# Moving the attention layer's splits and the rotation's sine products from GpSimd to VectorE

## The chip, the cores and the metric

One core of a Trainium2 chip runs the whole program. The metric is device time in microseconds (us), here of three runs of each kernel. Besides these there is one profiled execution, from which all rows of this document come. The engines are PE (TensorE, matmul; PEld is its weight load), DVE (VectorE), ACT (ScalarE), POOL (GpSimd) and SP (SyncE, which only issues DMAs here).

## The reference, cut to what matters

Two layers of a diffusion transformer over 1024 latent tokens and 256 context tokens, 1024 channels, all in fp32. The first layer mixes by a Fourier transform and gated linear attention, the second by grouped-query attention with rotary positions; each ends with a convolutional feed-forward block. The change touches only the second layer's attention:

```python
q_l = apply_rope(attn_q(a_lat, w_q, g_q[j]), cos, sin)
k_l, v_l = attn_kv(a_lat, w_kv, g_k[j])
k_l = apply_rope(k_l, cos, sin)
k_c, v_c = attn_kv(a_ctx, w_kv, g_k[j])
...
s = jnp.einsum('bkgqd,bksd->bkgqs', q, k).astype(jnp.float32) * (HEAD_DIM ** -0.5)
p = jax.nn.softmax(s, axis=-1).astype(v.dtype)
...
o_lat = ob.transpose(1, 0, 4, 2, 3, 5).reshape(B_, S, Q_WIDTH) @ w_att_out[j]
...
def apply_rope(t, cos, sin):
    t1, t2 = jnp.split(tf, 2, axis=-1)
    return jnp.concatenate([t1 * cos - t2 * sin, t1 * sin + t2 * cos], axis=-1).astype(t.dtype)
```

There are 8 query heads and 2 key/value heads of 128 channels; `attn_q` and the keys also pass an RMS norm per head.

## The kernel before

Every matmul factor is held as two fp32r parts, hi and lo, and each product is three matmuls (`mm3`, L518). The parts come from `split` (L206): ScalarE rounds the source to hi (the CAST on L208), then one subtraction gives lo, on VectorE unless the caller names GpSimd (`G`). All two-tensor operations are issued by the helper `tt`, so they stand on L204 in the profile whoever calls them.

```python
def tt(out_, a, b, op, eng=None):
    return (eng or V).tensor_tensor(out_, a, b, op)

def split(src, hi, lo, eng=None):
    A.copy(hi, src)
    return tt(lo, src, hi.bitcast(F32), ALU.subtract, eng)
```

The attention layer runs in this order; the times are from the span's start in the profiled execution.

- **Up to about 1692.** The first layer's feed-forward block ends. `att_split` (L1706) splits the normed input of one half of the tokens (640 columns, 8 channel blocks), its even blocks on GpSimd and its odd ones on VectorE. The keys and values of the first half follow.
- **1692 to 1831, the projection.** `kv` (L1795) and `q_all` (L1830) make keys and queries two heads at a time. `tok_w` (L536) loads and splits the weights, two pieces of 128x1024 per set, their lo on GpSimd. `heads2` (L1738) then works block by block: for each of its tiles of 128 tokens (3 tiles for queries of the first half, 5 elsewhere) 24 matmuls of 256 columns on TensorE; the copy and squares on ScalarE (L1748, L1750); the inverse root of all tiles' sums (L386 to L395, with a square root on ScalarE in between); per tile two scalings by it on VectorE (L1758), two products with the sines on GpSimd (L1762, L1763), two with the cosines and two sums on VectorE (L1764 to L1767); then two transposes per tile on TensorE (L1772). `staged` (L1776) issues the matmuls of a block ahead of the rest of the block before it. `parts` (L1802) splits the finished keys and values, 128x1280 each, their lo on GpSimd. `att_split` of the second half runs ahead of the fourth query block.
- **1831 to 2200, the attention.** For each of 8 heads and 2 query halves `att_open` (L1870) loads 512 queries and splits them, lo on GpSimd. `att_a` (L1883) makes scores, the maximum on VectorE (L1894), the exponential on ScalarE (L1896) and the final scaling on GpSimd (L1905); `att_b` (L1909) transposes the weights, splits them from PSUM on ScalarE and VectorE, and multiplies by the values.
- **Twice, near 2010 to 2075 and 2200 to 2280,** `att_out` (L1939) makes the output projection: 8 weight pieces of 128x1024, loaded and split by `Wt` (L215), lo on GpSimd, each with 24 matmuls of 512 columns. The second one overlaps the preparation of the next feed-forward block (`Norm.scale`, `ffn_ops`, `Up.split`), part of which is on GpSimd before and after the change.

No order is written by hand here. Each engine has one queue that it works off in order, and a list scheduler with priorities of the program's stretches (`stream`, L169) settles it when the program is built; a new placing of an operation thus moves its neighbours too. Pools of fixed slots (`S` of 31, `W` of 10) limit how far loads run ahead. All loads named here are issued on SP's queue.

Of the kernel before, what the change touches and what calls it, by code (L numbers as in the profile page):

```python
# [20 lines left out]
P = 128  # L21
# [83 lines left out]
def tile_hybrid_dit(  # L105
# [100 lines left out]
# [4 lines that stand above are left out]
# [1496 lines left out]
    def att_split(hf):  # L1706
        for k in range(KT):
            a_t[hf][k] = b = S((2, HALF), True)
            split(hp[hf][k // 2][:, k % 2], b[:, 0], b[:, 1], (G, V)[k % 2])
            if k % 2:  # L1710
                hp[hf][k // 2].free()
            yield
# [25 lines left out]
    def heads2(c, tiles, w2, gi, put):  # L1738

        a = a_get(c)  # L1740
        nt = len(tiles)
        us = []
        ss = SM(2 * nt)
        for i, t in enumerate(tiles):
            ps = tok_chunk(a, w2, t)
            u = S((4, 2, P))
            us.append(u)
            A.copy(u[:, 0], ps.rearrange("p (h d) -> p h d", h=2))  # L1748
            for h in range(2):
                A.activation(u[:, 3, h], ps[:, h * P:(h + 1) * P], AF.Square, scale=P ** -0.5,  # L1750
                             accum_out=ss[:, 2 * i + h:2 * i + h + 1])
        yield
        rst = SM(2 * nt)
        rsqrt(ss, 2 * nt, rst)
        for i, (t, u) in enumerate(zip(tiles, us)):
            q, o, w = u[:, 0], u[:, 1], u[:, 2]
            for h in range(2):
                V.scalar_tensor_tensor(q[:, h], q[:, h], rst[:, 2 * i + h:2 * i + h + 1], gqk[:, gi], ALU.mult, ALU.mult)  # L1758
            g = c * NT + t - 2
            if g >= 0:  # L1760
                cs, sn = [rope[:, g, j, :].unsqueeze(1).broadcast_to([P, 2, 64]) for j in range(2)]
                tt(w[:, :, 0:64], q[:, :, 64:P], sn, ALU.mult, G)  # L1762
                tt(w[:, :, 64:P], q[:, :, 0:64], sn, ALU.mult, G)  # L1763
                tt(o[:, :, 0:64], q[:, :, 0:64], cs, ALU.mult)  # L1764
                tt(o[:, :, 64:P], q[:, :, 64:P], cs, ALU.mult)
                tt(o[:, :, 0:64], o[:, :, 0:64], w[:, :, 0:64], ALU.subtract)
                tt(o[:, :, 64:P], o[:, :, 64:P], w[:, :, 64:P], ALU.add)  # L1767
        yield
        for h in range(2):
            ps = banks((4, 4), nt * P, 1 if nt <= 4 else 2)  # L1770
            for i, (t, u) in enumerate(zip(tiles, us)):
                PE.transpose(ps[:, i * P:(i + 1) * P], u[:, 1 if c * NT + t >= 2 else 0, h], ident)  # L1772
            put(h, ps)
        free(*us)
# [10 lines left out]
    with stream(8):  # L1785
        rt = S(1280)
        rope = rt[:, 0:1024].rearrange("p (g i d) -> p g i d", g=8, i=2)
        gqk = rt[:, 1024:1280].rearrange("p (i d) -> p i d", i=2)
        nc.scalar.dma_start(rope, k_rope)
        nc.scalar.dma_start(gqk[:, 0], g_q[0].partition_broadcast(P))  # L1790
        nc.scalar.dma_start(gqk[:, 1], g_k[0].partition_broadcast(P))
        k_f = [S(TOK) for _ in range(2)]
        v_f = [S((5, 256)) for _ in range(2)]

        def kv(c):  # L1795
            def put(h, ps):
                A.copy(k_f[h][:, c * HALF:(c + 1) * HALF], ps)
            wk = tok_w(w_qkv_v, 1024, 256, G)
            yield from heads2(c, range(NT), wk, 1, put)
            free(*wk)  # L1800

        def parts(b):  # L1802
            hi, lo = S(TOK, True), S(TOK, True)
            split(b.a, hi.a, lo.a, G)
            b.free()
            return hi, lo

        def v_w():
            return tok_w(w_qkv_v, 1280, 256, G)

        def vv(c, wv):
            for t in range(NT):
                ps = tok_chunk(a_get(c), wv, t)
                A.copy(v_f[c][:, t, :], ps)
            free(*wv)
            v_s.append(parts(v_f[c]))

        def q_block(i, w2, c):
            tiles = range(2, NT) if c == 0 else range(NT)
            n = len(tiles) * P  # L1820
            st = S((2, n))

            def put(h, ps):
                A.copy(st[:, h], ps)
            yield from heads2(c, tiles, w2, 0, put)
            o = HALF - CTX if c else 0
            DMA(qS[2 * i:2 * i + 2, :, o:o + n].rearrange("h p c -> p h c"), st.a)
            st.free()

        def q_all(c):  # L1830
            for i in range(4):
                w2 = tok_w(w_qkv_v, 256 * i, 256, G)
                if c == 0 and i == 3:
                    run(att_split(1))
                yield q_block(i, w2, c)
                free(*w2)

        run(a_gen)
        k_s, v_s = [], []
        def kv_q():  # L1840
            yield kv(1)
            q = q_all(1)
            yield next(q)
            k_s.extend(parts(b) for b in k_f)
            yield from q

        g = kv(0)
        next(g)
        wv = v_w()
        run(att_side(n_att[1]))  # L1850
        vv(0, wv)
        run(g)
        staged(q_all(0))
        free(*a_t[0])
        staged(kv_q())
        rt.free()
# [13 lines left out]
    def att_open(qb, h):  # L1870
        B = Blk()
        B.kv, B.h, B.qb = h // 4, h, qb
        if h % 2 == 0:
            o_s[qb, h // 2] = (S((2, 512), True), S((2, 512), True))
        qr = W(512)
        DMA(qr.a, qS[h, :, qb * 512:(qb + 1) * 512])
        B.qs = W((2, 512), True)
        split(qr.a, B.qs[:, 0], B.qs[:, 1], G)
        qr.free()
        B.pr, B.po = {}, {}  # L1880
        return B
# [57 lines left out]
    def att_out(qb, between=lambda n: None):  # L1939
# [4 lines left out]
        for n in range(KT):  # L1944
            if n % 2 == 0:
                DMA(hp[qb][n // 2].a, hS[n * P:(n + 2) * P, qb * 512:(qb + 1) * 512].rearrange("(k p) c -> p k c", p=P))
            h = hp[qb][n // 2][:, n % 2]
            w = Wt(w_ao_v[:, :, n * P:(n + 1) * P], (KT, P), G)
            ps = banks(TO, 512, 1)
            for k in range(KT):  # L1950
                oh, ol = o_s[qb, k // 2]
                mm3(ps, (w.hi[:, k, :], w.lo[:, k, :]), (oh[:, k % 2], ol[:, k % 2]), k == 0, k == KT - 1)
            w.free()
            V.scalar_tensor_tensor(h, ps, mods[:, 1, 2, n, 0:1], h, ALU.mult, ALU.add)
            dump("h3", h, (n, slice(None), slice(CTX + qb * 512, CTX + (qb + 1) * 512)))
            N.sq(n, N.acc_b.a, W)
            if n % 2:
                h_store(h3_d, qb, n // 2, 512)
            between(n)
# [147 lines left out]
```

## Time and profile before

| | us |
|---|---|
| runs (3): median, lowest to highest | 3030.18, 3023.17 to 3033.33 |
| profiled execution, its own time | 3020.81 |
| its span in the trace | 3018.9 |
| busy in the span: PE | 2770.2 |
| DVE | 2344.4 |
| ACT | 1440.7 |
| POOL | 985.9 |

The profiled execution lies 9.4 us under the median of the runs and 1.9 us over its span. The page gives busy time by engine; the views of the trace give the same for a stretch, for one line and shape, or in order of time. In such rows "idle before" is the time that the engine stood still just ahead of the instruction, with what released it. TensorE runs at a granted clock (PEclk, 1.00 is 2.4 GHz, its other level is 1.2 GHz), so a stretch at 0.90 has lost a tenth of its length to the clock.

### The profile page before, as it was taken

To read this page: it belongs to the slowest core of one execution; us is meant where nothing else is said; L and a number is where in the kernel's file an instruction comes from. 1 tells how busy PE (TensorE), PEld (TensorE's weight loads), DVE (VectorE), ACT (ScalarE), POOL (GpSimd) and SP (SyncE) were. 2 spreads that over 40 slices of the span, in tenths; PEclk is the share of its full clock that TensorE was granted. 3 is DMA by queue.
4 is the path that set the end of the run, shared out by engine and by line. 5 is a ranking of instruction groups with operands and counts; after the bars stand their busy time and mean duration, and the time that the engine had idled before them with its cause. 6 is when DMAs were issued, how large, how long until landed. Compare 5 with 4: busy or idle time off the path is not lost. (4 is left out here: it accounts for less than half of the span.)

```text
span 3018.9 us, 50383 instructions
## 1 busy us (share of the span) xinstructions
PE 2770.2 (92%) x19189; PEld 2601.9 (86%) x19189; DVE 2344.4 (78%) x4065; ACT 1440.7 (48%) x2892; POOL 985.9 (33%) x843
## 2 busy tenths in 40 slices
PE   5999988797899999999999889999987999999898
PEld 4899977797798999989899888998977999998677
DVE  7897479768877766677894788876878888888885
ACT  3544433535544444453354545764755455455343
POOL 2025275104332222123233654343344333232211
PEclk7999978998899999999899999999998999999999
DMA  8553302332343333459753220012042222227973
GB/s 282 183 159 104 114 32 79 96 127 66 99 127 124 128 121 116 131 173 305 230 172 126 88 88 29 15 58 73 12 123 68 80 85 74 78 81 230 289 242 111
DMA packets 375784, 371.18 MB, mean 123 GB/s; under 512 B 15579, under 2 KB 305011, under 8 KB 375540
## 3 DMA queue, kind: packets, MB, share of 16 engines
q1 hardware_dynamic: 374482, 365.88, 38.0%
q8 instruction: 151, 2.47, 0.3%
q10 hardware_dynamic: 1058, 2.07, 0.2%
q14 instruction: 93, 0.76, 0.1%
HBM read 282.95 MB, written 84.93 MB: 122 GB/s over the span
## 5 line engine op out<-in xcount | busy, mean ns | idle before, releaser
L154 PE MATMUL psum<-t,t 128*128 128x320 f32 (+4 forms) x17038 | 2575.5, 311 | 159.5 <-DVE t L204 88.4
L154 PEld LDWEIGHTS psum<-t,t 128*128 128x128 f32 x17038 | 2412.0, 194 | 286.0 <-DVE t L204 105.0
L204 POOL TENSOR_TENSOR t<-t,t 128x512 fp32r<-128x512 f32 (+8 forms) x499 | 736.4, 1492 | 1124.7 <-ACT t L208 856.9
L204 DVE TENSOR_TENSOR t<-t,t 128x512 fp32r<-128x512 f32 (+12 forms) x997 | 829.5, 863 | 195.2 <-ACT t L208 87.0
L208 ACT CAST t<-t 128x512 fp32r<-128x512 f32 (+5 forms) x857 | 553.2, 672 | 589.3 <-DVE t L204 185.8
L204 DVE TENSOR_TENSOR t<-t,psum 128x320 f32<-128x320 f32 (+5 forms) x408 | 201.8, 516 | 43.8 <-ACT t L1310 21.2
L204 DVE TENSOR_TENSOR t<-t 128x512 f32<-128x512 f32 (+3 forms) x263 | 164.8, 646 | 45.4 <-DMA t<-in_w_ffn_down_dram 31.7
L204 POOL TENSOR_TENSOR t<-t 128x320 f32<-128x320 f32 (+2 forms) x120 | 124.0, 1067 | 225.0 <-ACT t L664 157.2
L208 ACT CAST t<-psum 128x512 fp32r<-128x512 f32 (+4 forms) x248 | 130.9, 536 | 134.8 <-PE psum L158 60.2
L158 PE MATMUL psum<-ident,t 128*128 128x128 f32 (+2 forms) x955 | 151.1, 280 | 39.5 <-DVE t L204 23.5
L204 DVE TENSOR_TENSOR t<-psum,t 128x512 fp32r<-128x512 f32 (+4 forms) x248 | 151.4, 615 | 37.6 <-ACT t L208 34.7
L1316 POOL COPY halo<-t 128x4 f32<-128x4 f32 x44 | 8.3, 188 | 472.6 <-DVE t L204 472.6
L1905 POOL TENSOR_SCALAR t<-t,ring 128x640 f32<-128x640 f32 x128 | 101.7, 808 | 168.7 <-DVE ring L1895 79.1
L158 PEld LDWEIGHTS psum<-ident,t 128*128 128x128 f32 (+2 forms) x955 | 113.3, 143 | 48.9 <-DVE t L204 27.7
L1328 ACT ACTIVATE t<-t,cvs 128x639 f32<-128x639 f32 (+3 forms) x176 | 152.3, 866 | 0.6 <-issue 0.6
L918 DVE SCALAR_TENSOR_TENSOR t<-psum,mods,t 128x320 f32<-128x320 f32 (+3 forms) x182 | 88.3, 513 | 42.7 <-PE psum L154 39.8
L1894 DVE TENSOR_REDUCE ring<-psum 128x1 f32<-128x640 f32 x128 | 104.5, 818 | 19.4 <-PE psum L154 13.6
L1327 ACT ACTIVATE t<-t 128x511 f32<-128x511 f32 (+3 forms) x88 | 60.5, 688 | 119.1 <-DVE t L1332 93.4
L1896 ACT ACTIVATE t<-psum,ring 128x640 f32<-128x640 f32 x128 | 102.3, 800 | 23.8 <-DVE ring L1902 11.2
L1300 ACT COPY t<-psum 128x320 f32<-128x320 f32 (+1 forms) x88 | 35.3, 401 | 150.7 <-DVE t L204 102.4
L1336 DVE SCALAR_TENSOR_TENSOR t<-t,cvs,t 128x255 f32<-128x255 f32 (+1 forms) x66 | 54.0, 845 | 66.7 <-ACT t L1328 66.7
L1310 ACT COPY t<-psum 128x320 f32<-128x320 f32 (+1 forms) x88 | 35.1, 398 | 122.9 <-PE psum L154 122.7
(145 smaller groups left out, 1690.8 us busy)
## 6 DMA issues: line engine op xcount, KB each, us to landing
t<-in_w_ffn_up_dram SPq DMA_DIRECT2D x98, 512.0 KB, 3.9
ring<-in_w_mod_dram SPq DMA_DIRECT2D x56, 512.0 KB, 3.8
t<-in_w_ffn_down_dram SPq DMA_DIRECT2D x96, 256.0 KB, 6.0
t<-in_w_even_in_dram SPq DMA_DIRECT2D x28, 512.0 KB, 4.9
t<-in_w_ffn_down_dram SPq DMA_DIRECT2D x72, 192.0 KB, 2.7
t<-y_d SPq DMA_DIRECT2D x20, 640.0 KB, 6.4
t<-in_w_mod_dram SPq DMA_DIRECT2D x96, 128.0 KB, 2.2
t<-in_w_ffn_down_dram SPq DMA_DIRECT2D x24, 512.0 KB, 4.4
```

The costliest lines, as they stand in the source:

```text
L154: cls.keep(out_, nc.tensor.matmul(out_, *args, **kw).ins)
L158: cls.keep(out_, nc.tensor.transpose(out_, *args).ins)
L204: return (eng or V).tensor_tensor(out_, a, b, op)
L208: A.copy(hi, src)
L918: last_resid[0] = V.scalar_tensor_tensor(h[:, n % 2, a:b], ps[:, a - c0:b - c0], mods[:, l, m, n, v:v + 1], h[:, n % 2, a:b], ALU.mult, AL ...
L1300: copied[:] = [A.copy(C(0, 0), ps)]
L1327: order(copied[0], A.activation(us[0], us[0], AF.Silu))
L1328: order(copied[0], A.activation(x, c[:, j, at:at + m], AF.Identity, bias=tap(l, 3, ft), scale=tap(l, 1, ft)))
L1336: V.scalar_tensor_tensor(x[:, s0 + 1:e], c[:, j, 2 + s0:1 + e], tap(l, 0, ft), x[:, s0 + 1:e], ALU.mult, ALU.add)
L1894: V.tensor_reduce(mx[:, i:i + 1], ps, AX.XY, ALU.max)
L1896: A.activation(pt[:, i * HALF:(i + 1) * HALF].rearrange("p (b n) -> p b n", b=2), ps, AF.Exp, bias=nb[:, i:i + 1], scale=SCALE, accum_out= ...
L1905: G.tensor_scalar(pt[:, i * HALF:(i + 1) * HALF], pt[:, i * HALF:(i + 1) * HALF], ex[:, i:i + 1], 1.0, ALU.mult, ALU.mult)
```

## The change

Ten places drop the engine `G`, so that the subtraction or product goes to VectorE: 40 lo parts of weights of 128x1024 (24 pieces of the projection, 16 of the two output projections), 8 of the layer's input of 128x640, 4 of keys and values of 128x1280, 16 of queries of 128x512, and 80 products with the sines (two for each of 40 tiles of 128 tokens). Their casts on ScalarE, their loads and all arithmetic stay. In the attention layer GpSimd keeps the 128 scalings of L1905.

```diff
     def att_split(hf):
         for k in range(KT):
             a_t[hf][k] = b = S((2, HALF), True)
-            split(hp[hf][k // 2][:, k % 2], b[:, 0], b[:, 1], (G, V)[k % 2])
+            split(hp[hf][k // 2][:, k % 2], b[:, 0], b[:, 1])
...
-                tt(w[:, :, 0:64], q[:, :, 64:P], sn, ALU.mult, G)
-                tt(w[:, :, 64:P], q[:, :, 0:64], sn, ALU.mult, G)
+                tt(w[:, :, 0:64], q[:, :, 64:P], sn, ALU.mult)
+                tt(w[:, :, 64:P], q[:, :, 0:64], sn, ALU.mult)
...
-            wk = tok_w(w_qkv_v, 1024, 256, G)
+            wk = tok_w(w_qkv_v, 1024, 256)
...
-            split(b.a, hi.a, lo.a, G)
+            split(b.a, hi.a, lo.a)
...
-            return tok_w(w_qkv_v, 1280, 256, G)
+            return tok_w(w_qkv_v, 1280, 256)
...
-                w2 = tok_w(w_qkv_v, 256 * i, 256, G)
+                w2 = tok_w(w_qkv_v, 256 * i, 256)
...
-        split(qr.a, B.qs[:, 0], B.qs[:, 1], G)
+        split(qr.a, B.qs[:, 0], B.qs[:, 1])
...
-            w = Wt(w_ao_v[:, :, n * P:(n + 1) * P], (KT, P), G)
+            w = Wt(w_ao_v[:, :, n * P:(n + 1) * P], (KT, P))
```

GpSimd's queue around the first query blocks of the projection. A row names what is written and read: t_15484 is the lo part of the third block's first weight piece, t_15481 its raw values and t_15483 its hi; t_15284, t_15312 and t_15340 are the work tiles of the first block's three token tiles, t_14865 the table of cosines and sines.

```order
-L204 TENSOR_TENSOR t_15484<-t_15481,t_15483 128x1024
-L204 TENSOR_TENSOR t_15284<-t_15284,t_14865 128x2x64 x2
-L204 TENSOR_TENSOR t_15490<-t_15487,t_15489 128x1024
-L204 TENSOR_TENSOR t_15312<-t_15312,t_14865 128x2x64 x2
-L204 TENSOR_TENSOR t_15340<-t_15340,t_14865 128x2x64 x2
-L204 TENSOR_TENSOR t_15621<-t_15618,t_15620 128x1024
```

All of these leave GpSimd's queue, which has 536 rows after the change and 644 before.

VectorE's queue at the same place, the rotation of the first query block:

```order
 L204 TENSOR_TENSOR ring<-ring 128x6
+L204 TENSOR_TENSOR t_15490<-t_15487,t_15489 128x1024
 L1758 SCALAR_TENSOR_TENSOR t_15284<-t_15284,ring,t_14865 128x128 x2
 L1758 SCALAR_TENSOR_TENSOR t_15312<-t_15312,ring,t_14865 128x128 x2
 L1758 SCALAR_TENSOR_TENSOR t_15340<-t_15340,ring,t_14865 128x128 x2
-L204 TENSOR_TENSOR t_15284<-t_15284,t_14865 128x2x64 x2
-L204 TENSOR_TENSOR t_15312<-t_15312,t_14865 128x2x64 x2
-L204 TENSOR_TENSOR t_15340<-t_15340,t_14865 128x2x64 x2
+L204 TENSOR_TENSOR t_15284<-t_15284,t_14865 128x2x64 x4
+L204 TENSOR_TENSOR t_15312<-t_15312,t_14865 128x2x64 x4
+L204 TENSOR_TENSOR t_15340<-t_15340,t_14865 128x2x64 x4
```

The products per tile grow from two to four in one queue, and a weight split stands ahead of the block's scalings.

VectorE's queue at the start of the second output projection. t_21442 and t_21476 are lo parts of its third and fourth weight pieces, L1954 adds a finished piece to the residual, and the rows with psum belong to `Norm.scale` of the next feed-forward block:

```order
 L1124 TENSOR_SCALAR ring<-ident,ring 128x128 x4
+L204 TENSOR_TENSOR t_21442<-t_21439,t_21441 128x1024
 L1954 SCALAR_TENSOR_TENSOR t_21365<-psum,mods,t_21365 128x512
+L204 TENSOR_TENSOR t_21476<-t_21473,t_21475 128x1024
 L204 TENSOR_TENSOR t_19352<-t_19352,psum 128x1024
 L204 TENSOR_TENSOR t_19354<-t_19354,psum 128x1024
```

Two weight splits now stand in VectorE's queue ahead of that norm's multiplications.

## Rows read from the trace of the kernel before

**Rows 1.** The page, part 1: span, and busy time of each engine.
```profile
span 3018.9 us, 50383 instructions
PE 2770.2 (92%) x19189; PEld 2601.9 (86%) x19189; DVE 2344.4 (78%) x4065; ACT 1440.7 (48%) x2892; POOL 985.9 (33%) x843
```

**Rows 2.** Busy time by stage: start:end, length, five engines (instructions), PEclk, DMA share, GB/s.
```profile
1692.00:1751.00 59.00, 46.44 (x348) 45.56 (x347) 50.85 (x101) 27.62 (x96) 40.22 (x37) 0.88 0.32 100
1751.00:1831.00 80.00, 74.35 (x598) 72.52 (x597) 70.64 (x170) 35.44 (x129) 49.09 (x61) 0.96 0.23 77
1860.00:2010.00 150.00, 145.58 (x1130) 142.19 (x1129) 131.69 (x368) 104.84 (x251) 58.10 (x68) 1.00 0.09 29
2200.00:2310.00 110.00, 87.17 (x476) 74.62 (x476) 81.71 (x107) 58.04 (x96) 51.40 (x31) 0.90 0.34 102
```

**Rows 3.** TensorE's waits in 1692:1831, 2010:2110 and 2200:2310: total us, times, longest.
```profile
PE psum L158 <- DVE t L204: 17.9, 6, 4.9
...
PE psum L154 <- POOL t L204: 1.7, 1, 1.7
...
PE psum L154 <- POOL t L204: 10.7, 4, 5.9
PE psum L154 <- DVE t L204: 10.6, 3, 8.4
```

**Rows 4.** VectorE in order of time: start, length, line, shape, count [idle before].
```profile
1665.28 2.76 DVE L1758 SCALAR_TENSOR_TENSOR t<-t,ring,t 128x128 f32<-128x128 f32 x2
...
1668.94 2.19 DVE L1758 SCALAR_TENSOR_TENSOR t<-t,ring,t 128x128 f32<-128x128 f32 x8
...
1691.93 1.61 DVE L386 TENSOR_SCALAR ring<-ring 128x6 f32<-128x6 f32 x1 [11.67 <-ACT t L1750]
...
1750.76 0.17 DVE L386 TENSOR_SCALAR ring<-ring 128x10 f32<-128x10 f32 x1 [6.83 <-ACT t L1750]
...
1752.52 6.30 DVE L1758 SCALAR_TENSOR_TENSOR t<-t,ring,t 128x128 f32<-128x128 f32 x10
1758.75 2.90 DVE L204 TENSOR_TENSOR t<-t,t 128x128 f32<-128x128 f32 x10
1761.57 2.10 DVE L204 TENSOR_TENSOR t<-t 128x128 f32<-128x128 f32 x10
...
1767.17 8.89 DVE L1758 SCALAR_TENSOR_TENSOR t<-t,ring,t 128x128 f32<-128x128 f32 x10
1775.98 8.04 DVE L204 TENSOR_TENSOR t<-t,t 128x128 f32<-128x128 f32 x10
```

**Rows 5.** GpSimd in order of time, two of its stretches beside these.
```profile
1665.40 2.50 POOL L204 TENSOR_TENSOR t<-t,t 128x1024 fp32r<-128x1024 f32 x1 [12.08 <-ACT t L208]
...
1767.71 15.35 POOL L204 TENSOR_TENSOR t<-t,t 128x1024 fp32r<-128x1024 f32 x14 [7.63 <-ACT t L208]
```

**Rows 6.** VectorE's groups by line and shape, 1600 to 1840: busy, mean ns, idle before.
```profile
L1758 DVE SCALAR_TENSOR_TENSOR t<-t,ring,t 128x128 f32<-128x128 f32 x84 | 59.0, 769 | 0.4
L204 DVE TENSOR_TENSOR t<-t,t 128x128 f32<-128x128 f32 x80 | 32.1, 468 | 0.0
L204 DVE TENSOR_TENSOR t<-t 128x128 f32<-128x128 f32 x80 | 21.8, 331 | 0.4 <-POOL t L204 0.4
```

**Rows 7.** GpSimd's groups by line and shape, 1585 to 2290.
```profile
L204 POOL TENSOR_TENSOR t<-t,t 128x1024 fp32r<-128x1024 f32 x40 | 97.6, 2442 | 119.6 <-ACT t L208 93.1 <-PE psum L154 11.9 <-ACT t L1750 6.9
...
L204 POOL TENSOR_TENSOR t<-t,t 128x128 f32<-128x128 f32 x80 | 40.5, 536 | 7.5 <-DVE t L1758 6.9 <-ACT t L1750 0.5
L204 POOL TENSOR_TENSOR t<-t,t 128x640 fp32r<-128x640 f32 x8 | 14.4, 1799 | 2.5 <-ACT t L208 2.5
L204 POOL TENSOR_TENSOR t<-t,t 128x1280 fp32r<-128x1280 f32 x4 | 11.8, 2954 | 9.7 <-ACT t L208 9.7
```

**Rows 8.** VectorE's groups of the whole span, two shapes of split.
```profile
L204 DVE TENSOR_TENSOR t<-t,t 128x512 fp32r<-128x512 f32 x280 | 215.6, 781 | 14.4 <-ACT t L208 13.7
...
L204 DVE TENSOR_TENSOR t<-t,t 128x1024 fp32r<-128x1024 f32 x37 | 48.5, 1312 | 28.4 <-ACT t L208 26.6 <-ACT t L505 1.0 <-PE psum L154 0.8
```

## The prediction

> **What bounds the kernel now.** I read the page first, then busy time by stage, then TensorE's waits in the stages that the change touches, and only then VectorE and GpSimd in order of time. Over the span TensorE is busy 92%, VectorE 78%, GpSimd 33% [rows 1]: TensorE is the bound, and what can be won is where it stands still. In 1692 to 1751 it is busy 46.44 of 59 us at a granted clock of 0.88, in 1751 to 1831 74.35 of 80 us at 0.96 [rows 2]. Its own work at full clock is therefore 46.44 - 0.12 x 59 = 39.4 us and 74.35 - 0.04 x 80 = 71.2 us, 110.6 us of the 139. The other 28.4 us are waits (17.9 us, six times, all transposes behind VectorE's rotation [rows 3]) and clock granted at the lower level around them. In the second output projection, 2200 to 2310, TensorE waits 10.7 us for GpSimd (four times) and 10.6 us for VectorE [rows 3], at a clock of 0.90 [rows 2]; in the first one GpSimd holds it up once, 1.7 us [rows 3]. In the attention, 1860 to 2010, TensorE is busy 145.58 of 150 us [rows 2].
>
> **Why VectorE is late.** It looks full in 1692 to 1751 (50.85 of 59 us [rows 2]): from 1691.93 until 6.83 us before 1750.76 it hardly pauses [rows 4]. But its instructions are not of one length. Eight scalings of 128x128 (L1758) take 2.19 us, 0.274 each, when GpSimd idles; two take 2.76 us while GpSimd has one 128x1024 subtraction under way from 1665.40 to 1667.90 [rows 4, 5]. At 1767.17 ten scalings take 8.89 us and at 1775.98 ten cosine products 8.04 us, beside 14 GpSimd operations that fill 1767.71 to 1783.06 [rows 4, 5]; at 1758.75 the same ten products take 2.90 us (0.29 each), and ten sums 2.10 us (0.21 each) [rows 4]. So VectorE is held while GpSimd works. From 1600 to 1840 the 84 scalings were busy 59.0 us where 84 x 0.274 = 23.0 would do, the 80 cosine products 32.1 for 23.2, the 80 sums 21.8 for 16.8 [rows 6]: 36.0 + 8.9 + 5.0 = 49.9 us of being held, in three groups alone.
>
> The Trainium skill ("SBUF — State Buffer", section "Who interferes with whom") states this as a lock: of a VectorE instruction with two SBUF inputs and a GpSimd instruction that reads SBUF, the later is blocked for the whole of the other. The trace agrees (2.76 against 0.55 us for two scalings).
>
> **The change, part by part.** Against the profiled execution, 3020.8 us; the median of the runs, 3030.2, is 9.4 above it.
>
> *Projection, 1692 to 1831.* GpSimd loses its splits (2.44 us each for 128x1024, 1.80 for 128x640, 2.95 for 128x1280) and sine products (0.536 each) [rows 7], so nothing of GpSimd's is left there to hold VectorE. VectorE gains the same instructions at its own price: 1.31 us for a 128x1024 split [rows 8], scaled by columns 0.82 for 640 and 1.64 for 1280, and 0.29 for a sine product, which has the shape of the cosine product [rows 4]. Its work up to 1751 is then: 12 tiles of two scalings, four products and two sums, 24 x (0.274 + 0.29 + 0.29 + 0.21) = 25.5; four root chains at 1.76, the distance from 1750.76 to 1752.52 [rows 4], 7.0; and, as the new queue orders them between the first root and the first of five tiles, nine weight pieces, 11.8, and seven input splits, 5.7. That is 50.0 us. After 1751: five blocks of 10 x 1.064 + 1.76 = 12.4, so 62.0; six weight pieces 7.9, two key splits 3.3, two query splits 0.78 each [rows 8], 1.6; 74.8 us. Together 125 us, against 110.6 us for TensorE and 139 us taken now. VectorE becomes the bound, and 14 us go if it never pauses. The 1.76 hold some 0.5 us of waiting for ScalarE in which the new queue has other work (9 x 0.5), so that 19 us is possible; TensorE's own work caps it at 28. I take -16, near VectorE's sum because TensorE needs the rotation of one block only after the matmuls of later ones. Late next, where VectorE paces it: the same transposes.
>
> Ahead of 1692 VectorE is idle 11.67 us [rows 4]; six of the new splits (four pieces of weights, one of values, one of input) stand there, 4 x 1.31 + 1.64 + 0.82 = 7.7 us, and cost nothing. If that cover is short they join the 125 us. The weight loads stay on SP's queue; but a split that now heads VectorE's queue waits for the cast of its load and holds the rotations behind it. If each of the 15 weight pieces came late by a split's length, that would be 15 x 1.31 = 20 us, and the stage would end 20 - 14 = 6 us later than now; so its bounds are -28 and +6.
>
> *Attention, 1831 to 2200.* Sixteen query splits of 0.78 us [rows 8] come to VectorE, 12.5 us. It has 150 - 131.69 = 18.3 us free in 150 [rows 2], so some 45 in the 369. Bounds: 0 to +12.5 us. I take +1, as the room is over three times the load.
>
> *First output projection.* Eight splits of 1.31 instead of 2.44 us. The one wait of 1.7 us behind GpSimd [rows 3] shrinks by 1.13: -1 us (bounds 0 and -1.7).
>
> *Second output projection.* Also eight, VectorE now having 8 x 1.31 = 10.5 us more in a stretch where it was busy 81.71 of 110 us, partly held by GpSimd [rows 2]. Four waits behind a split that is 1.13 us shorter give -4.5. All of the 10.7 us and half of the clock's 0.10 x 110 = 11 us would give -16. The other end is above nothing: two pieces stand ahead of the norm's multiplications in VectorE's queue, and if their loads are late by a split's length each, it costs +2.6. I take -6, one short clock lapse saved besides the -4.5.
>
> Sum: -16 + 1 - 1 - 6 = **-22 us**: 2999 us for the profiled execution, and **3008 us** for the median.
>
> **The rivals.**
>
> *VectorE stays as late as it is.* It was busy 50.85 + 70.64 = 121.5 us in 1692 to 1831 [rows 2] and would carry 125 us: the hold is swapped for work of the same length. If its pauses stay too (17.5 us of the 139), the stage stays at 139 and only the output projections give up to 6 us: 3027. For it: both sums, and a rotation chain that now has four products in one queue. Against it: the pauses follow TensorE's own lateness (6.83 us before 1750.76 after a run of 52 us [rows 4]). The Trainium skill ("Perfetto Trace Analysis", section "Optimizing Scalar/DVE Operations") leans this way: as the two engines share an SBUF read port, moving work between them might not help. The held scalings show the port; whether the move helps no row shows.
>
> *VectorE's long instructions are its own.* If GpSimd is not what lengthens them, VectorE keeps the 49.9 us in three groups, and the 80 sine products take 0.468 as the cosine products' mean does [rows 6], 14.2 us more: up to 64 us on top of the 125. The break-even with 139 is at a share of 14 / 64, 22%. At half of it the stage takes 157 us, 18 more than now; with nothing from the projections that is 3048, *slower*. Against it stand the undisturbed runs of the same instructions [rows 4].
>
> *TensorE's own work is reached.* If the bound passes back to TensorE, the stage gives 28 us, the output projections 17: 2985.
>
> **How the numbers follow.** About 0.3%, 9 us, is what a measurement of this kernel can tell from no change. My forecast, a gain of 9 to 35 us, has 0.68, since each of its prices has an undisturbed row; TensorE's bound 0.08; VectorE as late as before 0.14; long instructions of its own 0.10. Faster is the first two, 0.76; same 0.14; slower 0.10. The range runs from 2988, most of the way to TensorE's bound, up to 3028, over the rival without a gain, and leaves out the slower case and a little below.
>
> **What would show it right or wrong.** Right: the scalings of L1758 at a mean near their undisturbed length (0.769 us now [rows 6]); no wait of TensorE behind GpSimd in the output projections; VectorE's busy time in the projection stage about as now, in a shorter stage; TensorE's waits there well under 17.9 us. Wrong: L1758 still long without GpSimd beside it; VectorE waiting on casts of weights ahead of a rotation; more of TensorE's waits behind VectorE in the attention than the page's stage shows now.

## The result and the profile after

Six runs of each kernel give 2992.82 us (2984.28 to 3000.87) after the change and 3028.19 us before (3023.17 to 3033.33): a ratio of 0.9882, 95% interval 0.9868 to 0.9895, or -35.4 us. The profiled executions differ by less, 2990.0 against 3018.9 us of span: the one of before lies 7.4 us under its kernel's median, the one of after 0.9 us.

The page of after, part 1, to be held against [rows 1]:

```profile
span 2990.0 us, 50271 instructions
PE 2760.4 (92%) x19189; PEld 2594.8 (87%) x19189; DVE 2337.0 (78%) x4213; ACT 1439.5 (48%) x2892; POOL 795.6 (27%) x695
```

VectorE runs 148 instructions more (the diff has nine edited lines, not ten) and is busy 7.4 us *less*; GpSimd loses 190 us. Busy time by stage, after (the projection, part of the attention, the second output projection; columns as in [rows 2]):

```profile
1692.00:1805.00 113.00, 113.00 (x962) 112.99 (x961) 100.68 (x377) 63.83 (x230) 0.00 (x0) 1.00 0.34 107
1827.00:1975.00 148.00, 144.59 (x1130) 141.87 (x1129) 130.90 (x379) 108.66 (x255) 49.12 (x62) 1.00 0.09 30
2166.00:2285.00 119.00, 91.83 (x530) 79.09 (x529) 94.69 (x129) 62.95 (x106) 38.18 (x25) 0.93 0.31 95
```

In the projection TensorE now works 113.00 of 113 us at the full clock, and the view of its waits has no row there; before, it was 139 us with 17.9 us of waits [rows 3]. VectorE needs 100.68 us of them, and GpSimd runs nothing. Its groups by line and shape in 1600 to 1820, after, against [rows 6, 7, 8]:

```profile
L204 DVE TENSOR_TENSOR t<-t,t 128x128 f32<-128x128 f32 x160 | 34.5, 281 | 0.0
L204 DVE TENSOR_TENSOR t<-t,t 128x1024 fp32r<-128x1024 f32 x24 | 29.3, 1220 | 14.3 <-ACT t L208 13.8 <-PE psum L154 0.4
L1758 DVE SCALAR_TENSOR_TENSOR t<-t,ring,t 128x128 f32<-128x128 f32 x84 | 22.9, 346 | 0.2
L204 DVE TENSOR_TENSOR t<-t 128x128 f32<-128x128 f32 x80 | 18.5, 280 | 0.0
```

The 84 scalings fall from 59.0 to 22.9 us; 160 products (cosines and sines) now take 34.5 us where 80 took 32.1. The means of short operations that follow each other overlap; the busy time divided by the count (0.22 us a product) is what one of them adds.

In order of time the same landmarks show where the 28.9 us of the spans come from. From the first of the keys' copies (L1748) to the first maximum of the scores (L1894) before takes 182.7 us (1650.71 to 1833.45) and after 153.2 (1651.92 to 1805.15): -29.5. The attention with the first output projection, up to the first addition of the second (L1954), gives -5.9, of which -1.7 lie in the first output projection (from its first addition on L1954 to its eighth, 44.7 to 42.9). The second one up to the next feed-forward block (its first copy on L1316) gives -1.4. That block and the final part give back 6.7, and ahead of the first landmark 1.2 were lost.

### The profile page after: what moved, and what is told of

The parts are those of the page before. It is cut to its first block, busy times and chain, and to the rows that moved or that the text cites. A ratio compares the mean times of both kernels' runs of the same rounds, so it can differ in the third digit from the quotient of the medians.

```text
span 2990.0 us, 50271 instructions
## 1 busy us (share of the span) xinstructions
PE 2760.4 (92%) x19189; PEld 2594.8 (87%) x19189; DVE 2337.0 (78%) x4213; ACT 1439.5 (48%) x2892; POOL 795.6 (27%) x695
## 5 line engine op out<-in xcount | busy, mean ns | idle before, releaser
L154 PE MATMUL psum<-t,t 128*128 128x256 f32 (+4 forms) x17038 | 2570.0, 310 | 157.5 <-DVE t L204 104.6
L204 DVE TENSOR_TENSOR t<-t,t 128x512 fp32r<-128x512 f32 (+13 forms) x1145 | 890.6, 810 | 228.2 <-ACT t L208 118.3
L208 ACT CAST t<-t 128x512 fp32r<-128x512 f32 (+4 forms) x857 | 552.9, 671 | 615.7 <-DVE t L204 197.4
L204 POOL TENSOR_TENSOR t<-t,t 128x512 fp32r<-128x512 f32 (+5 forms) x351 | 545.6, 1567 | 1018.5 <-ACT t L208 792.3
L1905 POOL TENSOR_SCALAR t<-t,ring 128x640 f32<-128x640 f32 x128 | 103.2, 820 | 434.7 <-DVE ring L1903 272.8
L158 PE MATMUL psum<-ident,t 128*128 128x128 f32 (+2 forms) x955 | 149.7, 278 | 22.9 <-DVE t L204 5.9
L1316 POOL COPY halo<-t 128x4 f32<-128x4 f32 x44 | 8.3, 188 | 474.7 <-DVE t L204 474.7
L1894 DVE TENSOR_REDUCE ring<-psum 128x1 f32<-128x640 f32 x128 | 104.5, 817 | 17.6 <-PE psum L154 16.6
```

What stands on the lines that cost most here:

```text
L154: cls.keep(out_, nc.tensor.matmul(out_, *args, **kw).ins)
L158: cls.keep(out_, nc.tensor.transpose(out_, *args).ins)
L1894: V.tensor_reduce(mx[:, i:i + 1], ps, AX.XY, ALU.max)
L1905: G.tensor_scalar(pt[:, i * HALF:(i + 1) * HALF], pt[:, i * HALF:(i + 1) * HALF], ex[:, i:i + 1], 1.0, ALU.mult, ALU.mult)
```

## The experiments

Theory A: VectorE is held while GpSimd runs instructions that read SBUF; once these are gone VectorE is early and TensorE's own work is left. The rivals change from run to run and stand in the expectations. "Projection" below is the time between the two landmarks, 182.7 us before and 153.2 after.

### Parts of the change

**e1_sines**: the kernel before, only the two sine products of a tile on VectorE.

```diff
-                tt(w[:, :, 0:64], q[:, :, 64:P], sn, ALU.mult, G)
-                tt(w[:, :, 64:P], q[:, :, 0:64], sn, ALU.mult, G)
+                tt(w[:, :, 0:64], q[:, :, 64:P], sn, ALU.mult)
+                tt(w[:, :, 64:P], q[:, :, 0:64], sn, ALU.mult)
```

> Only the 80 sine products go to VectorE; all splits stay on GpSimd. Theory A (GpSimd's work holds VectorE, and a late VectorE is what TensorE waits for): GpSimd keeps some 85 of its 125 us in the projection, so most of the holding stays; about 12 us faster than before, 3016, scalings of L1758 at a mean of 0.5 to 0.7 us. Theory B (TensorE waited for the sine products because they came late from GpSimd's queue): nearly all of the projection's gain, 25 us or more, 3003 or less, with L1758 still long.

Measured: 3022.29 us, ratio 0.9991 (0.9979 to 1.0004), projection 180.1 us. Groups of VectorE, and one of GpSimd, 1600 to 1855:

```profile
L1758 DVE SCALAR_TENSOR_TENSOR t<-t,ring,t 128x128 f32<-128x128 f32 x84 | 51.2, 678 | 0.7
L204 DVE TENSOR_TENSOR t<-t,t 128x128 f32<-128x128 f32 x160 | 33.9, 278 | 0.0
...
L204 POOL TENSOR_TENSOR t<-t,t 128x1024 fp32r<-128x1024 f32 x24 | 67.6, 2822 | 102.9 <-ACT t L208 66.9 <-PE psum L154 24.1 <-DVE ring L204 6.5
```

The products cost VectorE next to nothing (160 in the time that 80 took), so the long products of before were held, not long. But the splits that stay on GpSimd still meet the scalings, 678 ns each, and the time does not move, where theory A had forecast a gain of 12 us: the sine products alone are not the gain.

**e2_splits**: the other part of the projection; the changed kernel with the sine products, the query splits of the attention and the weights of the output projections back on GpSimd.

```diff
-                tt(w[:, :, 0:64], q[:, :, 64:P], sn, ALU.mult)
-                tt(w[:, :, 64:P], q[:, :, 0:64], sn, ALU.mult)
+                tt(w[:, :, 0:64], q[:, :, 64:P], sn, ALU.mult, G)
+                tt(w[:, :, 64:P], q[:, :, 0:64], sn, ALU.mult, G)
...
-        split(qr.a, B.qs[:, 0], B.qs[:, 1])
+        split(qr.a, B.qs[:, 0], B.qs[:, 1], G)
...
-            w = Wt(w_ao_v[:, :, n * P:(n + 1) * P], (KT, P))
+            w = Wt(w_ao_v[:, :, n * P:(n + 1) * P], (KT, P), G)
```

> Only the projection's splits (input, weights, keys, values) go to VectorE; sine products, query splits and output weights stay on GpSimd. Theory A: the longest holds (2.4 us each) are gone, 80 short ones of 0.5 us stay; about 20 us faster than before, 3008, L1758 at a mean of 0.35 to 0.5 us. Theory B: the sine products lose what was ahead of them in GpSimd's queue but stay there; 5 to 10 us faster, 3018 to 3023, TensorE still waiting for rotations.

Measured: 2995.9 us, ratio 0.9913 (0.9885 to 0.9941), projection 155.7 us. TensorE waits 0.5 us in 1692 to 1811. VectorE's groups in 1600 to 1855:

```profile
L1758 DVE SCALAR_TENSOR_TENSOR t<-t,ring,t 128x128 f32<-128x128 f32 x84 | 33.0, 462 | 0.3
L204 DVE TENSOR_TENSOR t<-t,t 128x1024 fp32r<-128x1024 f32 x24 | 30.5, 1272 | 6.9 <-ACT t L208 5.3 <-PE psum L154 1.4
L204 DVE TENSOR_TENSOR t<-t,t 128x128 f32<-128x128 f32 x80 | 23.0, 346 | 0.0
```

The splits of the projection are most of the gain, 12 us more than theory A gave them. The sine products still hold VectorE a little (scalings 462 ns against 346), but it has room for that. In the attention the run loses 6.7 us of its lead on before. Its query splits stand on GpSimd, but they do so before as well, so they don't explain this loss; the profiled execution is 8.3 us slower than the run's median, and the loss was not traced.

**e3_rest**: the kernel before with only the query splits and the weights of the output projections on VectorE.

```diff
-        split(qr.a, B.qs[:, 0], B.qs[:, 1], G)
+        split(qr.a, B.qs[:, 0], B.qs[:, 1])
...
-            w = Wt(w_ao_v[:, :, n * P:(n + 1) * P], (KT, P), G)
+            w = Wt(w_ao_v[:, :, n * P:(n + 1) * P], (KT, P))
```

> The kernel before with only the query splits of the attention and the weight splits of the two output projections on VectorE; the projection stays as it was, products with the sines and splits on GpSimd. Theory A (the gain of the change is made in the projection, where GpSimd held VectorE): the projection keeps its length of about 182 us from 1651 to the first scores, its waits of TensorE behind VectorE stay near 18 us, and the time falls by what the attention and the output projections gave in the changed kernel, some 7 us in the attention and first output projection, to about 3021 (3016 to 3026). Theory B (the attention and output projections carry the gain, because VectorE is held there too by GpSimd's splits): 3005 or less.

Measured: 3018.72 us, ratio 0.9985 (0.997 to 1.0), projection 182.3 us as before, scalings 766 ns. At the first addition of the second output projection the run is 5.1 us ahead of before, of which 0.1 was there when the attention began. So these edits by themselves make 5.0 of the changed kernel's -5.9, a gain and not the cost of +1 that was forecast.

**e4_out_back**: the changed kernel with the weights of the output projections on GpSimd.

```diff
-            w = Wt(w_ao_v[:, :, n * P:(n + 1) * P], (KT, P))
+            w = Wt(w_ao_v[:, :, n * P:(n + 1) * P], (KT, P), G)
```

> The changed kernel with the 16 weight splits of the output projections back on GpSimd. Theory A (in the second output projection moving them gained nothing: the waits behind GpSimd were swapped for one behind VectorE's queue, up to 9.3 us at 2209): the 9.3 us wait behind the lo part on VectorE goes, waits behind GpSimd of some 10 us as before return, time within 6 us of the changed kernel, 2990 to 2999. Theory B (the step gained, as the prediction had it with -6 and -1): 3000 or more. Theory C (the queue on VectorE costs, and the step would be better left on GpSimd): 2988 or less.

Measured: 2995.53 us, ratio 0.9909 (0.9891 to 0.9928); it overlaps with the changed kernel's 0.9868 to 0.9895. From the attention's start to the first addition of the second output projection it gains 6.5 us on before, with these weights on GpSimd: the gain there is that of the query splits. TensorE's waits in 2160 to 2305, first of the changed kernel:

```profile
PE psum L154 <- DVE t L204: 29.2, 12, 9.3
```

then of e4_out_back:

```profile
PE psum L154 <- DVE t L204: 18.2, 9, 8.4
PE psum L154 <- POOL t L204: 12.1, 4, 7.5
```

29.2 against 30.3 us: moving these sixteen splits swaps one kind of wait for another. The long one is seen in the changed kernel's TensorE and VectorE in order of time:

```profile
2209.00 16.18 PE L154 MATMUL psum<-t,t 128*128 128x512 f32 x72 [9.27 <-DVE t L204]
```

```profile
2202.75 3.39 DVE L204 TENSOR_TENSOR t<-t,t 128x512 fp32r<-128x512 f32 x2
2206.07 1.75 DVE L204 TENSOR_TENSOR t<-t 128x512 f32<-128x512 f32 x1
2207.74 1.21 DVE L204 TENSOR_TENSOR t<-t,t 128x1024 fp32r<-128x1024 f32 x1
...
2209.47 3.09 DVE L204 TENSOR_TENSOR t<-t,t 128x512 fp32r<-128x512 f32 x5
```

The weight split at 2207.74 stands behind subtractions of the next block's preparation that take 1.7 us each, where five of the same shape take 3.09 us at 2209.47. GpSimd's row of that time:

```profile
2202.66 4.61 POOL L204 TENSOR_TENSOR t<-t,t 128x512 fp32r<-128x512 f32 x3 [1.64 <-ACT t L208]
```

### What holds VectorE

**e5_ghost**: the changed kernel, and GpSimd repeats subtractions (hi minus hi; 32 in the trace, not the 36 of the expectation) and the 80 sine products into a scratch slot that nobody reads. Nothing that the projection computes depends on GpSimd, and from 1692 to 1862 no engine waits for it.

```diff
+    def ghost(hi, n):
+        h = hi.bitcast(F32)
+        for c in range(0, n, 1280):
+            e = min(n, c + 1280)
+            tt(scr[:, 0:e - c], h[:, c:e], h[:, c:e], ALU.subtract, G)
...
+                for a in (0, 64):
+                    tt(scr[:, 0:P].rearrange("p (h d) -> p h d", h=2), q[:, :, a:a + 64], sn, ALU.mult, G)
```

> The changed kernel, and besides GpSimd does again, on the same operands' hi parts and work tiles, 36 subtractions and 80 sine products whose results nobody reads (those of the first half's input are left out). Theory A: VectorE's scalings are long again (L1758 at 0.7 us or more), TensorE waits 15 us or more for VectorE in the projection, and since VectorE also has the work itself the time is 15 to 45 us over the changed kernel: 3008 to 3038. Theory B, and any theory by which only who computes the results and in which order counts: 2993, within 5 us, L1758 at 0.35.

Measured: 3045.38 us, ratio 1.0071 (1.0046 to 1.0097), slower than before and 7 us beyond theory A's range. Busy time in the projection, and VectorE's groups (the scalings stand on L1771 here):

```profile
1692.00:1862.00 170.00, 129.58 (x983) 127.10 (x982) 162.75 (x378) 66.51 (x234) 95.52 (x105) 0.86 0.23 74
```

```profile
L204 DVE TENSOR_TENSOR t<-t,t 128x128 f32<-128x128 f32 x148 | 59.9, 470 | 0.0
L1771 DVE SCALAR_TENSOR_TENSOR t<-t,ring,t 128x128 f32<-128x128 f32 x84 | 45.0, 606 | 0.3
```

VectorE's 378 instructions take 162.75 us, against 100.68 for the 377 of the changed kernel. TensorE's waits behind it come back, 39.4 us, and the granted clock falls to 0.86.

**e6_memset**: the same, with each ghost replaced by a subtraction of one column and zero fills, which write but don't read.

```diff
+    def ghost(hi, n):
+        tt(scr[:, 0:1], hi.bitcast(F32)[:, 0:1], hi.bitcast(F32)[:, 0:1], ALU.subtract, G)
+        for _ in range(2):
+            G.memset(scr[:, 0:n], 0.0)
...
+                for a in (0, 64):
+                    tt(scr[:, 0:1], q[:, 0, a:a + 1], q[:, 0, a:a + 1], ALU.subtract, G)
+                    G.memset(scr[:, 0:512], 0.0)
```

> As the run with idle repetitions, but GpSimd only reads one column of the same operand and then fills the scratch tile with zeros (two memsets of the split's width, or one of 512 columns for a sine product). Theory A with the detail that only a GpSimd instruction that reads SBUF holds VectorE's second input: L1758 at 0.35 to 0.4 us, time within 5 us of the changed kernel, 2988 to 2998. Theory A without that detail (any GpSimd access holds): L1758 at 0.5 us or more and 5 to 30 us slower than the changed kernel. Theory B: 2993, within 5 us, L1758 at 0.35.

Measured: 3042.58 us, ratio 1.0057 (1.0029 to 1.0085): the forecast of the time missed. But the instructions of VectorE are not held: scalings 346 ns, products 283. The time went elsewhere. GpSimd, with 93 subtractions of one column at 832 ns beside its fills, was busy 152.36 of 166 us, and ScalarE waited 38.3 us for it before it could overwrite the tiles that those subtractions read. So the run answers for the durations and not for the time; a lighter one was needed.

**e7_light**: as e6_memset, with one column and three fills on every second tile, one column and two fills for every second weight piece.

```diff
+    def ghost(src, n, times):
+        tt(scr[:, 0:1], src, src, ALU.subtract, G)
+        for _ in range(times):
+            G.memset(scr[:, 0:n], 0.0)
...
+                if t % 2 == 0:
+                    ghost(q[:, 0, 0:1], 512, 3)
...
+            ghost(ws[0].hi_b.t.rearrange("p k c -> p (k c)").bitcast(F32)[:, 0:1], 4 * w, 2)
```

> The changed kernel with GpSimd given lighter work that only writes: on every second tile of the rotation one subtraction of a single column and three zero fills of 128x512, for every second weight piece of the projection one such column and two fills of 128x1024, some 75 us in all, into a scratch slot that nobody reads. Theory A in detail (VectorE is held only by GpSimd instructions that read SBUF, not by GpSimd being busy): scalings of the rotation stay near 0.35 us and products near 0.28, the projection stays within 5 us of the changed kernel's 153 us, time 2990 to 3003. Theory B (any GpSimd work in the stage, or any slot used up by it, costs the gain): scalings above 0.5 us, or the projection 170 us or more, time 3010 or more.

Measured: 2999.4 us, ratio 0.9915 (0.9895 to 0.9934). Busy time in the projection, and the groups of VectorE and GpSimd (the scalings on L1766):

```profile
1692.00:1813.00 121.00, 115.67 (x961) 114.91 (x960) 100.84 (x371) 63.79 (x229) 92.61 (x102) 0.97 0.31 100
```

```profile
L204 DVE TENSOR_TENSOR t<-t,t 128x128 f32<-128x128 f32 x160 | 34.6, 289 | 0.0
L1766 DVE SCALAR_TENSOR_TENSOR t<-t,ring,t 128x128 f32<-128x128 f32 x84 | 23.1, 347 | 0.3
...
L204 POOL TENSOR_TENSOR t<-t 128x1 f32<-128x1 f32 x37 | 56.1, 1517 | 74.4 <-DVE t L1766 52.4 <-ACT t L208 19.8
L214 POOL MEMSET t<- 128x512 f32 x75 | 39.6, 528 | 4.4
L214 POOL MEMSET t<- 128x1024 f32 x24 | 22.9, 954 | 1.4
```

GpSimd is busy 92.61 us of this stage, nearly as long as in e5_ghost (95.52), and VectorE takes 100.84 us, as in the changed kernel. About half of the 92.61 us are fills; the other half are the one-column subtractions, most of it time in which GpSimd itself is held. GpSimd and then VectorE in order of time:

```profile
1757.36 0.19 POOL L204 TENSOR_TENSOR t<-t 128x1 f32<-128x1 f32 x1
1757.61 1.97 POOL L214 MEMSET t<- 128x1024 f32 x2
1759.67 10.21 POOL L204 TENSOR_TENSOR t<-t 128x1 f32<-128x1 f32 x1
```

```profile
1757.50 2.72 DVE L1766 SCALAR_TENSOR_TENSOR t<-t,ring,t 128x128 f32<-128x128 f32 x10
...
1769.32 0.50 DVE L204 TENSOR_TENSOR t<-t 128x128 f32<-128x128 f32 x2
1769.73 0.18 DVE L391 TENSOR_SCALAR ring<-ring 128x10 f32<-128x10 f32 x1
```

Ten scalings beside the two fills take 2.72 us, the same as ten with GpSimd idle (at 1738.57 of the changed kernel, shown below). The subtraction at 1757.36 takes 0.19 us; the one at 1759.67 takes 10.21 and ends at 1769.88, when VectorE's unbroken run of operations with two inputs has reached one with a single input (1769.73). So it waited for the end of a run of over thirty operations, and not of a single one. In e6_memset such subtractions took up to 8.38 us each.

The projection, 163.3 us, is 10 us longer than the changed kernel's and so outside the 5 us forecast; 5.4 us of that are waits of TensorE, on ScalarE and VectorE. GpSimd's instructions read whole tiles in e5_ghost, and one column or nothing here. That it is the reading, and no other difference between a subtraction and a zero fill, was not tried apart. The Trainium skill ("SBUF — State Buffer", section "Who interferes with whom") says so of a VectorE instruction with two SBUF inputs: it contends with a GpSimd instruction that reads SBUF, not with one that only writes it. The two runs agree (606 and 347 ns a scaling).

### Further along the same line

**e0_after**, **e8_ops** and **e8_again**: the changed kernel again, and (twice) the changed kernel with the last splits of the feed-forward inputs on VectorE too. The second time both ran on the same chip.

```diff
-            put("B21", p, b21[p], G)
+            put("B21", p, b21[p], V)
...
-            put("B22", p, b22[p], G)
+            put("B22", p, b22[p], V)
...
-                put("T3", p, t3, G)
+                put("T3", p, t3, V)
...
-                put("T3", p, b12[p], G)
+                put("T3", p, b12[p], V)
```

> The changed kernel, and also the splits of the feed-forward blocks' inputs that are still on GpSimd (B21, B22 and T3 of the operand preparation, which stands beside the second output projection) on VectorE; the splits of the feed-forward weights stay on GpSimd. Theory A (VectorE is held by GpSimd's splits of 128x512 there, and that makes the weight splits in its queue late): the wait of 9.3 us near 2209 shrinks below 6, and the time falls by 3 to 10 us against the changed kernel, to 2983 to 2990. Theory B (VectorE's queue is what makes them late, held or not; more work in it makes it worse): no gain or a loss, 2993 to 3005.

> The changed kernel again, beside the next two on the same chip, so that they are compared with it directly: 2988 to 2999 by every theory.

> The kernel of e8_ops again (the changed kernel with the feed-forward blocks' input splits also on VectorE), beside the changed kernel: if its gain is one of the kernel it is 8 to 16 us faster than the changed kernel here too, 2976 to 2986; if the earlier difference came from the chip, within 5 us of it.

Measured: e8_ops 2980.13 us, ratio 0.9849 (0.9826 to 0.9871), a little beyond theory A's range; e8_again 2976.57 us, 0.9835 (0.9817 to 0.9853), against 2992.45 us, 0.989 (0.9869 to 0.991) for the changed kernel on that chip: 15.9 us less. Of the mechanism that was named only a part shows: the wait that was 9.3 us near 2209 lies between two additions 11.9 us apart, where it was 17.4 (L1954), but a wait of 9.1 us stands elsewhere in the stage, and the sum behind VectorE falls from 29.2 to 21.6 us, with 3.3 us behind GpSimd that were not there. Against the first profile of the changed kernel, e8_ops leads by 0.4 us at 734, by 5.9 at 777, at the same step of the first feed-forward block, which this edit also touches, by 3.1 at 2248, by 6.7 at 2352, and by 9.5 at the end.

**e9_allv**: e8_ops, and all splits of the feed-forward blocks' first weights on VectorE. **e10_we**: also those of the second weights.

```diff
-                split(src[a], b[:, 0], b[:, 1], V if a in ON_V else G)
+                split(src[a], b[:, 0], b[:, 1], V)
...
-    WE = ((G, G, V), (V, G, V))
+    WE = ((V, V, V), (V, V, V))
```

The first pair of lines is e9_allv, both are e10_we.

> The kernel of e8_ops, and also all splits of the feed-forward weights (128x512, 1.5 us each on GpSimd) on VectorE at some 0.69 us each; GpSimd keeps work outside the splits. Theory A (a GpSimd instruction that reads SBUF costs VectorE about as much as doing the work itself): VectorE's busy time stays within 30 us of 2328 us although it takes over some 260 splits, and the time falls by 3 to 15 us against e8_ops, to 2965 to 2977. Theory B (in the feed-forward blocks, where TensorE is busy 97 to 98%, GpSimd's help is worth its holds): VectorE's busy time rises by over 80 us and the time is 2980 to 3010.

> The kernel of e9_allv, and also the last 84 splits of 128x512 on GpSimd, those of the weights of the feed-forward blocks' second product, on VectorE. Theory A (each such split costs VectorE as much as it saves, wherever it stands): VectorE's busy time stays within 15 us of 2308 us and the time falls by 3 us or more, to 2953 or less. Theory B (they stand mostly where the loads of weights set the pace, DMA engines 80 to 93% busy near 1400 to 1500 and 2700 to 2800, and VectorE is not late there): within 5 us of e9_allv, 2952 to 2961, with VectorE's busy time up to 30 us higher or lower.

Measured: e9_allv 2956.49 us, ratio 0.9772 (0.9754 to 0.979), 36.0 us under the changed kernel on the same chip and 8.5 us beyond theory A's range; e10_we 2952.18 us, 0.9763 (0.974 to 0.9785), which can't be told from e9_allv. Part 1 of the page of e9_allv:

```profile
span 2952.2 us, 49988 instructions
PE 2752.3 (93%) x19189; PEld 2590.7 (88%) x19189; DVE 2308.4 (78%) x4433; ACT 1445.1 (49%) x2892; POOL 464.8 (16%) x475
```

VectorE runs 220 instructions more than in the changed kernel and is busy 28.6 us less. What they cost comes back in what was held, as in two groups of 2300 to 2700, the changed kernel first, then e9_allv:

```profile
L204 DVE TENSOR_TENSOR t<-t,t 128x512 fp32r<-128x512 f32 x61 | 51.2, 839 | 0.4 <-ACT t L208 0.4
...
L1338 DVE SCALAR_TENSOR_TENSOR t<-t,cvs 128x511 f32<-128x511 f32 x18 | 30.0, 1665 | 0.6
```

```profile
L204 DVE TENSOR_TENSOR t<-t,t 128x512 fp32r<-128x512 f32 x150 | 102.2, 692 | 22.3 <-ACT t L208 22.3
...
L1338 DVE SCALAR_TENSOR_TENSOR t<-t,cvs 128x511 f32<-128x511 f32 x19 | 14.2, 746 | 0.0
```

In e10_we the 84 further splits add 5.6 us to VectorE's busy time (2314.0 us), within theory A's bound; its time is too near to e9_allv to say whether they gain. Both are clear of the changed kernel, and so beat both kernels of this case.

## Why the prediction was right, and where it was off

3008 us were predicted in a range of 2988 to 3028, with 0.76 for faster; it is faster, at 2992.8 us, in the range and near its fast end. That it lies there is in part luck. The steps missed in both directions: the projection gave 13.5 us more than forecast and the attention 5.1, while the second output projection gave 4.6 less and 7.9 us were lost in stretches that the forecast had at nothing. Step by step:

- **VectorE is held while GpSimd works: right.** The scalings went from 769 to 346 ns. That they are held by what GpSimd runs, and not by its being busy as such or by waiting for its results, is shown by e5_ghost and e7_light; that the reading is what counts is the nearest account of the two, with the limit said there.
- **Projection, -16 us with VectorE as the new bound: the mechanism right, the term mis-sized.** It gave -29.5 us, the case of the third rival, which had a chance of 0.08: TensorE's own work was reached (113.00 busy of 113 us, where 110.6 had been worked out). So a sign of being right failed too: VectorE's busy time in the stage, foreseen about as before (121.5 us), fell. The step that failed is VectorE's sum of 125 us; it measured 100.68. A product was taken at 0.29 us from the ten at 1758.75 as if they were undisturbed, but GpSimd was still at work beside them:

From the kernel before, GpSimd in order of time:

```profile
1752.85 7.24 POOL L204 TENSOR_TENSOR t<-t,t 128x1024 fp32r<-128x1024 f32 x11 [1.99 <-ACT t L208]
```

It ends at 1760.09, inside their 2.90 us. Undisturbed, after:

```profile
1737.06 0.16 DVE L386 TENSOR_SCALAR ring<-ring 128x10 f32<-128x10 f32 x1
1737.49 0.22 DVE L392 RECIPROCAL ring<-ring 128x10 f32<-128x10 f32 x1 [0.28 <-ACT ring L391]
1737.74 0.38 DVE L204 TENSOR_TENSOR ring<-ring 128x10 f32<-128x10 f32 x2
1738.15 0.17 DVE L395 TENSOR_SCALAR ring<-ring 128x10 f32<-128x10 f32 x1
1738.36 0.17 DVE L204 TENSOR_TENSOR ring<-ring 128x10 f32<-128x10 f32 x1
1738.57 2.72 DVE L1758 SCALAR_TENSOR_TENSOR t<-t,ring,t 128x128 f32<-128x128 f32 x10
1741.20 3.32 DVE L204 TENSOR_TENSOR t<-t,t 128x128 f32<-128x128 f32 x16
```

Sixteen products take 3.32 us, 0.21 each; over 37 tiles of four that is 37 x 4 x 0.08 = 12 us less. The root chain spans 1.5 us from 1737.06 to 1738.57, not 1.76, and only 1.10 of it are busy: 9 x 0.66 = 6 us less. That is 18 of the 24 us. A split takes 1.22 and not 1.31 us, but sixteen of 128x1024 stand in the stage and not fifteen (19.5 us, where 19.7 were priced). The rest is mostly that separate prices count twice what overlaps where one group's operations follow another's: the groups of the stage add up to 108.2 us, and VectorE is busy 100.68. The scalings, 2.72 us for ten, are as priced, though their price came from a row that GpSimd overlapped as well (1668.94 to 1671.13; GpSimd starts at 1670.16): there it did no harm.
- **Attention, +1: wrong in sign.** With the first output projection it gave -5.9, and -4.1 without. Sixteen query splits were counted as a load on VectorE, and the hold that the same splits on GpSimd put on VectorE was left out, though the projection had been argued from just that. The hold is there, in VectorE's smallest operations with two inputs (245 to 261 ns on average in the three kernels with these splits on GpSimd; 207 to 222 in the changed kernel, e0_after, e3_rest and e4_out_back). The group in 1835 to 2030 before, then in 1807 to 1998 after:

```profile
L204 DVE TENSOR_TENSOR ring<-ring 128x1 f32<-128x1 f32 x78 | 20.1, 257 | 0.9
```

```profile
L204 DVE TENSOR_TENSOR ring<-ring 128x1 f32<-128x1 f32 x78 | 16.1, 207 | 0.9
```

TensorE's waits on the exponentials fell from 6.8 us (1831 to 2010 before) to 2.9 us (1805 to 1980 after); that the hold is why is argued, not shown. e3_rest shows the gain without the rest of the change. Its size is less sure: from the first maximum to the first addition of the second output projection the three kernels with these splits on GpSimd take 382.6 to 389.5 us (before 382.9), the eleven others 374.4 to 383.9.
- **First output projection, -1: right**, -1.7 by the additions, and no wait behind GpSimd is left. But with these weights on GpSimd (e4_out_back) it takes 43.9 us, and in a second profile of the changed kernel 43.3, so about half of the -1.7 can be put down to this step.
- **Second output projection, -6: too good.** It gave -1.4. The four waits behind GpSimd did go, and waits behind VectorE took their place, up to 9.3 us at once (8.4 before [rows 3]). The prediction had that as two pieces late by one split each, +2.6; it left out that GpSimd's other splits, which the change leaves there, hold what stands ahead of the weights in VectorE's queue; e8_ops bears out only part of this.
- **The rivals.** "VectorE stays as late as it is" fell: it was busy 100.68 us in the stage and TensorE did not wait. Its sum of 3027 us counts half of the 6 us that it names. The rule beside it, of the Trainium skill ("Perfetto Trace Analysis", section "Optimizing Scalar/DVE Operations"), that offloading work between these two engines might not help, is said there of relieving a full VectorE; in this case the move the other way, off GpSimd, did help: the time became 0.9882 of before, and with further moves 0.9772. "VectorE's long instructions are its own" fell with the 346 ns.

What stays open is the second feed-forward block, where the changed kernel's two profiles, and those of e4_out_back, e7_light and e3_rest, lose 3 to 4 us of their lead from its start to its last step (2251.6 to 2710.6 in the changed kernel), and that of e2_splits loses none. Nothing edited stands there and it was not tried apart; e8_ops and e8_again, one and the same kernel, differ by 3.1 us over this stretch, so single profiles can hardly settle it.

## What to carry to other kernels

Price an operation on GpSimd by what it does to VectorE, too: here VectorE took over 148 instructions and then 220 more, and its busy time fell both times. An instruction's own length is safely read only where the other engine's rows show it idle for the whole of the row, not for a part. And a moved split joins the receiver's queue: in the second output projection the waits behind GpSimd became waits behind VectorE of about the same sum (29.2 us against 30.3).

## What was not expected of the hardware

- The hold runs both ways. A GpSimd subtraction of a single column took 0.19 us or 10.21 us in e7_light, by what VectorE ran beside it (rows above); its means, 832 ns in e6_memset and 1517 ns in e7_light, are mixtures of the two. In e1_sines GpSimd's 128x1024 subtraction took 2822 ns on average, against 2442 ns [rows 7], because two of them, near 1733 and 1811, took 5.33 and 8.57 us.
- Two profiles of the changed kernel reach the first edited stage 6.6 us apart (1651.9 and 1658.5 us), 4.8 us of which were there at 735, before any edited line; both then take 153.2 us for it. So single profiles compare the length of this stage far more closely than they compare end times.
